# LayerNorm sums by ones matmuls, a convolution block projected one place earlier, and the transposes of y in another kind of PSUM bank

## The chip, the cores and the metric

One core of a Trainium2 chip. The metric is device microseconds of one execution of the whole program. Engines are named as in the profile: PE (TensorE matmuls; PEld its weight loads), DVE (VectorE), ACT (ScalarE), POOL (GpSimd), SP (SyncE). The kernel before takes 1667.99 us, median of 3 runs (1667.68 to 1668.74).

## The reference, cut to what matters

```python
u = rmsnorm(h, norm_mix_w)                      # h: 16 meta tokens + 512 tokens, 1024 wide
z, xbc, dt_raw, conf_in = split(u @ w_in)       # ONE input projection
y_ssd = ssd_mixer(z, xbc, dt_raw, ...)          # conv of 4 taps, chunked scan, gate, RMSNorm by group
a, g = split(conf_in, 2)
c = causal_depthwise_conv(a * sigmoid(g), conf_conv_w, conf_conv_b)     # 31 taps, 1024 channels
mu = mean(c, axis=-1); var = mean((c - mu) ** 2, axis=-1)               # over the 1024 channels
y_conf = silu((c - mu) * rsqrt(var + EPS) * ln_g + ln_b)                # LayerNorm, swish
h = h + concatenate([y_ssd, y_conf]) @ w_out    # ONE output projection
h = h + peer_ffn(rmsnorm(h, norm_ffn_w), ...)   # 8 heads, top 16 of 128 x 128 single-neuron experts
out = rmsnorm(h, norm_final_w)[16:]
```

All arrays are float32.

## The kernel before, in words

Every matmul operand is split in a high and a low part, and a product is three matmuls, `mm3` (L160, L161, L162: high by high, high by low, low by high). The input projection is cut into 20 blocks that go over PE in the order of the string `ORDER`: `z0` to `z3` (gates of the SSD groups), `x0` to `x7` (x, B and C of the SSD), `c0` to `c7` (the 8 blocks of 128 channels of the convolution branch). As soon as the blocks of an SSD group are there, `ssd(g)` is written, ahead of other work (priority 2000); it works in PSUM banks of the kind "pb" (4 of them), the projection in banks of the kind "pa" (4).

`c_block(k)` projects block k in two halves (272 and 256 columns each), forms the GLU on ACT and DVE (L415, L416), and runs the 31 taps as 30 DVE instructions of 128x512 (L422), written with low priority. A copy of the mean of block 0 (`crow`) is subtracted from each block (L424); block 0's mean over channels comes from 4 ones matmuls (L428): the block's 128x128 pieces are the weights, and one column of ones is what moves through. The LayerNorm needs, for each token, the sum over all 1024 channels of the block values and of their squares. Blocks 0 to 6 are added up by DVE, in `sumd` (L439) and `sumq` (L438), 128x512 each; the squares are made by ACT (L436). At the end, in the part that begins at L679 (priority 500), 16 ones matmuls (L683) reduce `sumd`, `sumq`, block 7 and block 7's square over partitions; L685 to L693 turn that into the factors, `to_rows` (L402) spreads them over the partitions, and for each block DVE (L704, L705) and ACT (L706 Silu, L707 copy) make the normalised rows that the output projection reads.

The output projection `out_part(bs)` runs over the 4 quarters of w_out's rows, in two halves of columns (hf): `out_part([0])`, `out_part([1])` for the SSD's half, `out_part([2, 3])` for the convolution's. A quarter and half is 16 `mm3` of 512 columns (48 matmuls), in 4 "pa" banks by token tile t; L660 adds a finished bank to `h1`. Its weights come through `wsplit`: ACT copies the high part (L184) and its negative (L185) into one of two slots, and a DMA that POOL issues (L186) adds the raw weights onto it, which leaves the low part. Slots are used in turn, so the weights of `[1]`, hf 0 go into the slot that `[0]`, hf 0 has read. The y of the SSD comes back from DRAM (`yD`, issued by SP) and is transposed on PE by `y_split` (L620) into a "pa" bank; ACT (L626) and DVE (L627) split it.

The order on each engine is made when the program is built, by a scheduler that goes by priorities and its own cost estimates; on the chip each engine takes its instructions in that order, and waits for what the next one needs.

Of the kernel before, what the change touches and what calls it, by code (L numbers as in the profile page):

```python
# [15 lines left out]
AF = mybir.ActivationFunctionType  # L16
OP = mybir.AluOpType
# [4 lines left out]
D = 1024  # L22
# [18 lines left out]
NT = 4  # L41
HOLD = 2
TB = 8
ORDER = "z0 c0 x4 c1 x5 x6 c2 x7 x0 z1 x1 c3 c4 z2 x2 c5 z3 x3 c6 c7".split()
YP = 300
MO = (0, 1, -1, 2, 3)

# [65 lines left out]
F0 = S0 + 9728  # L113
L0 = F0 + 4240
# [3 lines left out]
def body(ctx, tc, I, out):  # L118
    nc = tc.nc
    V, S, G, E = nc.vector, nc.scalar, nc.gpsimd, nc.tensor  # L120
# [7 lines left out]
    def ps(tag="pb"):  # L128
        return psp.tile([128, 512], F32, name=tag, tag=tag)

    def early(n):
        return tc.high_priority(offset=n)

    def late(n):
        return tc.high_priority(offset=-n)

    def mem(a, n):
        assert a + n <= SLAB
        return M[:, a:a + n]
# [7 lines left out]
    def con(n):  # L147
        a = cp[0]
        cp[0] += n
        assert cp[0] <= W0, cp[0]  # L150
        return M[:, a:a + n]
# [64 lines left out]
    raws = []  # L216
    worder = [{"z": k - 1, "x": 3 + k, "c": 11 + k}[o] for o, k in ((o[0], int(o[1])) for o in ORDER) if (o, k) != ("z", 0)]

    def next_w():
        while worder and len(raws) < 2:  # L220
            src = I["win"][worder.pop(0)].rearrange("p j c n -> p (j c n)")
            raws.append((wload(src), src))
        raw, src = raws.pop(0)
        return wsplit(raw, src, parts=2)
# [10 lines left out]
    ones = con(128)  # L235
# [12 lines left out]
    def stat(n):  # L248
        a = stp[0] % 128
        if a + n > 128:  # L250
            a = 0
        stp[0] = a + n
        return st[:, a:a + n]

    def rstd_of(ss, n, scale, parts=128):
        v = stat(n)[:parts]
        V.tensor_scalar(v, ss, scale, EPS, op0=OP.mult, op1=OP.add)  # L257
        r = stat(n)[:parts]
        G.tensor_tensor(r, v, neghalf[:parts, :n], op=OP.pow)  # L259
        return r  # L260
# [11 lines left out]
    dtraw = con(80)  # L272
# [19 lines left out]
    for n, t in enumerate(MO):  # L292
        src, c0, parts = (xt[t], NM + 128 * t, 128) if t >= 0 else (xm, 0, NM)
# [6 lines left out]
        for half in range(2):  # L300
            hs = slice(512 * half, 512 * half + 512)
            V.scalar_tensor_tensor(u[:, hs], src[:parts, hs], r, wmix[:parts, hs], op0=OP.mult, op1=OP.mult)
            p = ps("pa" if n % 2 else "pb")
# [8 lines left out]
    def proj_ct(wh, wl, j):  # L312
        p0, p1 = ps("pa"), ps("pa")
        for dc in range(8):
            sh = wh[:, j * 1024 + dc * 128:j * 1024 + dc * 128 + 128]
            sl = wl[:, j * 1024 + dc * 128:j * 1024 + dc * 128 + 128]
            f, l = dc == 0, dc == 7
            mm3(p0[:, :272], sh, sl, uTh[:, dc, 0:272], uTl[:, dc, 0:272], f, l)
            mm3(p1[:, :256], sh, sl, uTh[:, dc, 272:528], uTl[:, dc, 272:528], f, l)
        return p0, p1  # L320
# [64 lines left out]
    convo = mem(V0, 4096).rearrange("p (c t) -> p c t", c=8)  # L385
    glu = [mem(F0 + 544 * k, 544) for k in range(4)]
    sig = mem(F0 + 2176, 528)
    atmp = [mem(F0 + 2704 + 512 * k, 512) for k in range(2)]
    cwh = con(248)
    V.tensor_scalar(cwh, small[:, S_CW:S_CW + 248], 0.5, None, op0=OP.mult)  # L390
    crow = mem(L0, 512)
    sumd = mem(L0 + 512, 512)
    sumq = mem(L0 + 1024, 512)
    assert L0 + 1536 <= SLAB
    ccol = con(4)
    atn = [0]
    sq7 = []

    def to_rows(cols):
        p = ps()  # L400
        for t in range(4):
            E.matmul(p[:, 128 * t:128 * t + 128], cols[:, t:t + 1].to_broadcast([128, 128]), ident,  # L402
                     start=True, stop=True)
        return p

    def c_block(k):
        wh, wl = next_w()
        g0, g1 = proj_ct(wh, wl, 0)
        S.activation(sig[:, 0:272], g0[:, :272], AF.Tanh, scale=0.5)
        S.activation(sig[:, 272:528], g1[:, :256], AF.Tanh, scale=0.5)  # L410
        a0, a1 = proj_ct(wh, wl, 1)
        gl = glu[k % 4]
        if k < 4:
            V.memset(gl[:, 0:14], 0.0)
        V.scalar_tensor_tensor(gl[:, 14:286], sig[:, 0:272], 1.0, a0[:, :272], op0=OP.add, op1=OP.mult)  # L415
        V.scalar_tensor_tensor(gl[:, 286:542], sig[:, 272:528], 1.0, a1[:, :256], op0=OP.add, op1=OP.mult)  # L416
        o = convo[:, k, :]
        cw = cwh[:, 31 * k:31 * k + 31]
        with late(LOWP):
            S.activation(o, gl[:, 0:512], AF.Identity, scale=cw[:, 0:1], bias=small[:, S_CB + k:S_CB + k + 1])  # L420
            for j in range(1, 31):
                V.scalar_tensor_tensor(o, gl[:, j:j + 512], cw[:, j:j + 1], o, op0=OP.mult, op1=OP.add)  # L422
            if k > 0:
                V.tensor_tensor(o, o, crow, op=OP.subtract)  # L424
            if k == 0:
                p = ps()
                for t in range(4):
                    E.matmul(p[:, t:t + 1], o[:, 128 * t:128 * t + 128], ones[:, 0:1], start=True, stop=True)  # L428
                V.tensor_scalar(ccol, p[:, 0:4], 1.0 / 128, None, op0=OP.mult)
                S.activation(crow, to_rows(ccol), AF.Copy)  # L430
                V.tensor_tensor(o, o, crow, op=OP.subtract)
                S.activation(sumq, o, AF.Square)
            else:
                at = atmp[atn[0] % 2]
                atn[0] += 1
                S.activation(at, o, AF.Square)  # L436
                if k < 7:
                    V.tensor_tensor(sumq, sumq, at, op=OP.add)  # L438
                    V.tensor_tensor(sumd, convo[:, 0, :] if k == 1 else sumd, o, op=OP.add)  # L439
                else:  # L440
                    sq7.append(at)


    sm = con(80 * 12)
# [144 lines left out]
    left = [0, 1, 2, 3]  # L589
    for o in ORDER:  # L590
        {"z": z_block, "x": x_block, "c": c_block}[o[0]](int(o[1]))
# [10 lines left out]
    def hl(kk):  # L602
        g = RG[kk // 4]
        return g[0][:, kk % 4, :], g[1][:, kk % 4, :]
# [10 lines left out]

    def y_split(src, t, g0, n):
        ts = slice(128 * t, 128 * t + 128)
        p = ps("pa")
        for d in range(2 * n):
            E.transpose(p[:, d * 128:d * 128 + 128], src[:, d * 128:d * 128 + 128], ident)  # L620
        for d in range(2 * n):
            kk = 2 * g0 + d
            wc = small[:, S_NW + kk:S_NW + kk + 1]
            pd = p[:, d * 128:d * 128 + 128]
            hh, ll = hl(kk)
            S.activation(hh[:, ts], pd, AF.Copy, scale=wc)  # L626
            V.scalar_tensor_tensor(ll[:, ts], pd, wc, hh[:, ts].bitcast(F32), op0=OP.mult, op1=OP.subtract)  # L627
# [49 lines left out]


    with early(LNP):  # L679
        p = ps()  # L680
        for c0, src in ((0, sumd), (4, sumq), (8, convo[:, 7, :]), (12, sq7[0])):
            for t in range(4):
                E.matmul(p[:, c0 + t:c0 + t + 1], src[:, 128 * t:128 * t + 128], ones[:, 0:1], start=True, stop=True)  # L683
        mom = stat(8)
        V.tensor_scalar(mom, p[:, 0:8], 1.0 / D, None, op0=OP.mult)  # L685
        V.scalar_tensor_tensor(mom, p[:, 8:16], 1.0 / D, mom, op0=OP.mult, op1=OP.add)
        dl = mom[:, 0:4]
        vv = stat(4)
        V.tensor_tensor(vv, dl, dl, op=OP.mult)
        V.tensor_tensor(vv, mom[:, 4:8], vv, op=OP.subtract)  # L690
        rst = rstd_of(vv, 4, 1.0)
        rho = stat(4)
        V.tensor_tensor(rho, dl, rst, op=OP.mult)  # L693
        prh = to_rows(rho)
        prs = to_rows(rst)
        pin = tc.keep_in_program_order

        def low(k):
            ch, cl = hl(k)
            pin(V.tensor_tensor(cl, convo[:, k, :], ch.bitcast(F32), op=OP.subtract))  # L700

        for k in range(8):
            cv = convo[:, k, :]
            pin(V.tensor_tensor(cv, cv, prs, op=OP.mult))  # L704
            pin(V.tensor_tensor(cv, cv, prh, op=OP.subtract))  # L705
            S.activation(cv, cv, AF.Silu, bias=small[:, S_LB + k:S_LB + k + 1], scale=small[:, S_LG + k:S_LG + k + 1])  # L706
            S.activation(hl(k)[0], cv, AF.Copy)  # L707
            if k > 1:
                low(k - 2)
        low(6)  # L710
        low(7)
# [4 lines left out]
    for t in range(4):  # L716
        x2 = x2s if t == 3 else mem(P0 + 1024 + 1024 * (t % 2), 1024)
# [107 lines left out]
    for h in range(8):  # L825
        wh, wl = split_n(raw_n(I["wq"][h].rearrange("p c n -> p (c n)"), 2048), 2048, V)
        for f in range(2):
            pq = ps("pa")
            for dc in range(8):
                o = dc * 256 + f * 128  # L830
# [4 lines left out]
            for t in range(4):  # L835
                E.matmul(psc[:, 128 * t:128 * t + 128], qT[:, 128 * t:128 * t + 128], keys[:, 2 * h + f, :],
                         start=True, stop=True)
# [258 lines left out]
```

## Time and profile before

| | us |
|---|---|
| runs (3): lowest, median, highest | 1667.68, 1667.99, 1668.74 |
| the profiled execution: its own time | 1670.01 |
| its span (first to last instruction) | 1668.2 |
| PE busy | 1619.8 (97%) |
| DVE busy | 1396.2 (84%) |
| ACT busy | 772.9 (46%) |
| POOL busy | 397.4 (24%) |
| mean granted TensorE clock | 0.988 |

Times in the trace count from the span's start. A timeline row gives start, duration, engine, line, operation, its output and input, and the count; in brackets stands the time that the engine sat idle before it and who released it. Several equal instructions in a row are one line; a matmul of plain float32 operands (the ones matmuls) stands there as two instructions, a transpose as one. The duration of a pipelined instruction is longer than the distance to the next one's start, which is the price used here. Granted clock 1.00 is 2.4 GHz, 0.50 is 1.2 GHz. The input projection fills about the first 298 us, the SSD's tail and the output projection follow to about 430 us, and the retrieval takes the rest.

### The profile page before, as it was taken

Reading aid. Unit: us, or ns where it says so; the run is one execution under the profiler, and the core shown is the slowest. Engines: PE = TensorE matmul, PEld = TensorE weight load, DVE = VectorE, ACT = ScalarE, POOL = GpSimd, SP = SyncE. Lnnn points to the kernel's source line nnn. Section 1 sums busy time; section 2 is a strip of 40 time slices with the busy share of each in tenths; the row PEclk is TensorE's granted clock in tenths of the full one; section 3 lists DMA queues with packets and bytes.
Section 4 is the critical chain, followed back from the end, with each engine's and each line's share of the span. In section 5 each row is a group of like instructions: output and inputs, shape, how many; then the busy total and the mean of one; then the engine's idle time right before and its main releaser. Section 6 shows DMA issues by size and latency. Waiting matters only on the chain. (4 is left out here: it accounts for less than half of the span.)

```text
span 1668.2 us, 26169 instructions
## 1 busy us (share of the span) xinstructions
PE 1619.8 (97%) x9529; PEld 1470.6 (88%) x9529; DVE 1396.2 (84%) x2864; ACT 772.9 (46%) x1179; POOL 397.4 (24%) x348
## 2 busy tenths in 40 slices
PE   7999999888899999999999999999999999999997
PEld 7999999767788999999999988888888899999996
DVE  5999899994579999999997478888888788988876
ACT  5566566536333344676766333333333333333332
POOL 1111111012000012022223232222222355454430
PEclk9999999988999999999999999999999999999999
DMA  7877576656222466799998889999999899999982
GB/s 218 191 169 170 130 162 156 201 132 143 82 92 80 136 190 233 221 338 340 331 332 316 293 291 367 348 344 349 349 337 350 303 343 354 355 357 361 338 309 89
DMA packets 166913, 425.38 MB, mean 255 GB/s; under 512 B 14576, under 2 KB 81392, under 8 KB 161664
## 3 DMA queue, kind: packets, MB, share of 16 engines
q1 hardware_dynamic: 121568, 261.17, 45.1%
q0 software_dynamic: 45216, 162.55, 32.2%
q8 instruction: 74, 1.21, 0.3%
q14 instruction: 55, 0.45, 0.1%
HBM read 381.72 MB, written 41.94 MB: 254 GB/s over the span
## 5 line engine op out<-in xcount | busy, mean ns | idle before, releaser
L160 PE MATMUL pa<-MR 128*128 128x512 f32 (+3 forms) x2120 | 726.9, 344 | 9.0 <-ACT MR L707 3.0
L161 PE MATMUL pa<-MR 128*128 128x512 f32 (+3 forms) x2120 | 726.2, 343 | 0.0
L162 PE MATMUL pa<-MR 128*128 128x512 f32 (+3 forms) x2120 | 687.7, 344 | 1.2 <-DVE MR L267 1.1
L160 PEld LDWEIGHTS pa<-MR 128*128 128x128 f32 x2120 | 402.1, 190 | 40.1 <-ACT MR L707 3.3
L162 PEld LDWEIGHTS pa<-MR 128*128 128x128 f32 x2120 | 401.3, 189 | 32.2 <-DVE MR L267 1.3
L161 PEld LDWEIGHTS pa<-MR 128*128 128x128 f32 x2120 | 401.8, 190 | 30.0 <-DVE MR L267 0.5
L788 ACT ACTIVATE MR<-M 128x1024 fp32r<-128x1024 f32 (+1 forms) x264 | 286.0, 1084 | 294.3 <-PE pa L161 107.1
L789 DVE TENSOR_TENSOR MR<-M,MR 128x1024 fp32r<-128x1024 f32 (+1 forms) x264 | 330.6, 1254 | 75.0 <-ACT MR L788 70.1
L929 POOL DMA_INDIRECT M<-wd,M x128 | 160.7, 1256 | 545.6 <-DVE M L945 280.3
L929 POOL DMA_INDIRECT M<-wu,M x128 | 164.0, 1281 | 313.9 <-DVE M L952 269.9
L161 PE MATMUL pb<-MR 128*128 128x384 f32 (+1 forms) x576 | 206.8, 359 | 0.0
L160 PE MATMUL pb<-MR 128*128 128x384 f32 (+1 forms) x576 | 206.3, 359 | 0.0
L162 PE MATMUL pb<-MR 128*128 128x384 f32 (+1 forms) x576 | 204.2, 359 | 0.0
L1016 ACT ACTIVATE MR<-M 128x384 fp32r<-128x384 f32 x128 | 67.0, 523 | 272.9 <-issue 203.2
L422 DVE SCALAR_TENSOR_TENSOR M<-M 128x512 f32<-128x512 f32 x240 | 174.5, 750 | 3.9 <-ACT M L420 3.0
L952 DVE SCALAR_TENSOR_TENSOR M<-M 128x1024 f32<-128x1024 f32 x128 | 163.8, 1279 | 14.0 <-DMA M<-wu,M 13.8
L945 DVE SCALAR_TENSOR_TENSOR M<-M 128x1024 f32<-128x1024 f32 x128 | 154.1, 1219 | 9.6 <-DMA M<-wd,M 9.6
L1017 DVE TENSOR_TENSOR MR<-M,MR 128x384 fp32r<-128x384 f32 x128 | 71.2, 556 | 59.6 <-ACT MR L1016 58.9
L160 PEld LDWEIGHTS pb<-MR 128*128 128x128 f32 x576 | 108.1, 188 | 11.4
L161 PEld LDWEIGHTS pb<-MR 128*128 128x128 f32 x576 | 108.1, 188 | 11.3
L162 PEld LDWEIGHTS pb<-MR 128*128 128x128 f32 x576 | 108.1, 188 | 10.7
L991 ACT ACTIVATE M<-pb 128x512 f32<-128x512 f32 x96 | 99.0, 1160 | 37.5 <-PE pb L989 37.5
(221 smaller groups left out, 1494.3 us busy)
## 6 DMA issues: line engine op xcount, KB each, us to landing
M<-wdT SPq DMA_DIRECT2D x128, 512.0 KB
M<-wu SPq DMA_DIRECT2D x128, 512.0 KB
GD<-M SPq DMA_DIRECT2D x40, 512.0 KB
M<-GD SPq DMA_DIRECT2D x32, 640.0 KB
M<-win SPq DMA_DIRECT2D x19, 1024.0 KB
MR<-win POOLq DMA_DIRECT2D x38, 512.0 KB
HD<-M SPq DMA_DIRECT2D x88, 192.0 KB
M<-HD SPq DMA_DIRECT2D x88, 192.0 KB
```

Of the source, the lines that this page charges most:

```text
L160: E.matmul(o, lh, rh, start=first, stop=False)
L161: E.matmul(o, lh, rl, start=False, stop=False)
L162: E.matmul(o, ll, rh, start=False, stop=last)
L422: V.scalar_tensor_tensor(o, gl[:, j:j + 512], cw[:, j:j + 1], o, op0=OP.mult, op1=OP.add)
L788: S.activation(wh, raw, AF.Copy)
L789: leng.tensor_tensor(wl, raw, wh.bitcast(F32), op=OP.subtract)
L929: r = G.indirect_dma_start(out=g, out_offset=None, in_=src, in_offset=bass.IndirectOffsetOnAxis(ap=e3[:, k:k + 1], axis=0))
L945: use(V.scalar_tensor_tensor(g, g, 1.0, x2s, op0=OP.mult, op1=OP.mult, accum_out=dots[:, k:k + 1]))
L952: use(V.scalar_tensor_tensor(h1[3], g, act3[:, k:k + 1], h1[3], op0=OP.mult, op1=OP.add))
L991: S.activation(gb.rearrange("p i t -> p t i")[:, c:c + 4, :], p.rearrange("p (t i) -> p t i", t=4), AF.Copy, scale=1.0 / GS)
L1016: S.activation(sh, sf, AF.Copy)
L1017: V.tensor_tensor(sl, sf, sh.bitcast(F32), op=OP.subtract)
```

## The change

Three edits. `c2` stands one place earlier in `ORDER`, ahead of `x6`. The 12 DVE adds (L438, L439) go: `block_sums(k)` reduces each block and its square by 8 ones matmuls into one column each, and a small DVE instruction adds the 128x8 result into `mom`; it is written two blocks later, in `c_block(k + 2)`, for blocks 0 to 5, and at the LayerNorm for 6 and 7. Four buffers for the squares instead of two take the place of `sumd` and `sumq`. `y_split` transposes into a "pb" bank. Lines behind the edits shift: L402 is now L399, L415 L412, L422 L419, L436 L429, L706 L701, L707 L702; the ones matmul is L437, its DVE instructions L439 and L441.

```diff
-ORDER = "z0 c0 x4 c1 x5 x6 c2 x7 x0 z1 x1 c3 c4 z2 x2 c5 z3 x3 c6 c7".split()
+ORDER = "z0 c0 x4 c1 x5 c2 x6 x7 x0 z1 x1 c3 c4 z2 x2 c5 z3 x3 c6 c7".split()
...
-    atmp = [mem(F0 + 2704 + 512 * k, 512) for k in range(2)]
+    atmp = [mem(o, 512) for o in (F0 + 2704, F0 + 3216, L0 + 512, L0 + 1024)]
...
-    sumd = mem(L0 + 512, 512)
-    sumq = mem(L0 + 1024, 512)
+    mom = dtraw[:, 0:8]
...
-                S.activation(sumq, o, AF.Square)
-            else:
-                at = atmp[atn[0] % 2]
-                atn[0] += 1
-                S.activation(at, o, AF.Square)
-                if k < 7:
-                    V.tensor_tensor(sumq, sumq, at, op=OP.add)
-                    V.tensor_tensor(sumd, convo[:, 0, :] if k == 1 else sumd, o, op=OP.add)
-                else:
-                    sq7.append(at)
+            S.activation(atmp[k % 4], o, AF.Square)
+            if k > 1:
+                block_sums(k - 2)
+
+    def block_sums(k):
+        p = ps()
+        for c0, src in ((0, convo[:, k, :]), (4, atmp[k % 4])):
+            for t in range(4):
+                E.matmul(p[:, c0 + t:c0 + t + 1], src[:, 128 * t:128 * t + 128], ones[:, 0:1], start=True, stop=True)
+        if k == 0:
+            V.tensor_scalar(mom, p[:, 0:8], 1.0 / D, None, op0=OP.mult)
+        else:
+            V.scalar_tensor_tensor(mom, p[:, 0:8], 1.0 / D, mom, op0=OP.mult, op1=OP.add)
...
     def y_split(src, t, g0, n):
         ts = slice(128 * t, 128 * t + 128)
-        p = ps("pa")
+        p = ps("pb")
...
     with early(LNP):
-        p = ps()
-        for c0, src in ((0, sumd), (4, sumq), (8, convo[:, 7, :]), (12, sq7[0])):
-            for t in range(4):
-                E.matmul(p[:, c0 + t:c0 + t + 1], src[:, 128 * t:128 * t + 128], ones[:, 0:1], start=True, stop=True)
-        mom = stat(8)
-        V.tensor_scalar(mom, p[:, 0:8], 1.0 / D, None, op0=OP.mult)
-        V.scalar_tensor_tensor(mom, p[:, 8:16], 1.0 / D, mom, op0=OP.mult, op1=OP.add)
+        block_sums(6)
+        block_sums(7)
```

The new order moves instructions in three places. The first is PE at the end of the input projection (L160 to L162 with 272 and 256 columns are the last matmuls of block c7's projection, L536 to L563 the SSD's). Before, transposes of y (L620) stand between the projection's matmuls:

```order
L162 MATMUL pa<-MR 128x256
L620 MATMUL pa<-M 128x128 x2
L160 MATMUL pa<-MR 128x272
L620 MATMUL pa<-M 128x128 x2
L161 MATMUL pa<-MR 128x272
...
L563 MATMUL pb<-M 128x256
L536 MATMUL pb<-M 128x128
L561 MATMUL pb<-M 128x64 x4
```

Of the changed kernel, what stands behind the projection and the SSD's last attention matmuls but two, down to the output projection's first matmuls:

```order
L437 MATMUL pb<-M 128x1 x16
L559 MATMUL pb<-M 128x256
L561 MATMUL pb<-M 128x64 x4
L620 MATMUL pb<-M 128x128 x6
L160 MATMUL pa<-MR 128x512
L161 MATMUL pa<-MR 128x512
```

All transposes of y now come behind the whole projection, and two blocks' ones matmuls (16 instructions) stand ahead of the first of them. Ahead of c7's last projection matmul there are 32 more ones matmuls than before, 4 transposes fewer, and 14 matmuls of the SSD (2 of L536, 1 L539, 4 L542, 1 L559, 4 L561, 2 L563) that stood behind it before.

The second place is PE in the output projection. The number behind `pa` is the bank's generation. Before, `[0]`, hf 1 ends (pa_3661), the transposes for quarter 1 follow, and then `[1]`, hf 0 begins (pa_3778), 48 matmuls after the last matmul that reads the weights of `[0]`, hf 0:

```order
L160 MATMUL pa_3661<-MR_64 128x512
L161 MATMUL pa_3661<-MR_64 128x512
L162 MATMUL pa_3661<-MR_64 128x512
L620 MATMUL pa_3719<-M_63 128x128 x2
...
L620 MATMUL pa_3771<-M_63 128x128 x2
L160 MATMUL pa_3778<-MR_64 128x512
L161 MATMUL pa_3778<-MR_64 128x512
```

Now the last matmul of `[0]`, hf 0 (into pa_3649) stands in the third quarter of hf 1 (pa_3706 to pa_3709), and the first of `[1]`, hf 0 is pa_3826:

```order
L161 MATMUL pa_3708<-MR_64 128x512
L162 MATMUL pa_3649<-MR_64 128x512
L162 MATMUL pa_3708<-MR_64 128x512
...
L620 MATMUL pb_3791<-M_63 128x128 x2
L620 MATMUL pb_3798<-M_63 128x128 x2
L620 MATMUL pb_3805<-M_63 128x128 x2
L160 MATMUL pa_3709<-MR_64 128x512
...
L160 MATMUL pa_3826<-MR_64 128x512
L160 MATMUL pa_3827<-MR_64 128x512
```

33 matmuls stand from hf 1's first one to the one into pa_3649, and 20 matmuls and 10 transposes behind it before the low part of `[1]`'s weights is needed. From there to the LayerNorm's spreading matmuls there are 80 matmuls with 512 columns and 16 ones matmuls, and 12 more matmuls behind the spreading.

The third place is ACT at the LayerNorm. Before, the squares (L436), splits of quarter 2 (L184, L185), the load of the table for Silu (L706), and then pairs of Silu and copy:

```order
L184 ACTIVATE MR<-M 128x512
L185 ACTIVATE MR<-MR 128x512 x2
L706 ACT_TABLE_LOAD
L706 ACTIVATE M<-M 128x512
L707 ACTIVATE MR<-M 128x512
L706 ACTIVATE M<-M 128x512
```

Now splits of quarter 3, whose slot is that of `[1]`, hf 1, stand ahead of the table load, between it and the first copy:

```order
L185 ACTIVATE MR<-MR 128x512 x2
L184 ACTIVATE MR<-M 128x512 x2
L185 ACTIVATE MR<-MR 128x512
L701 ACT_TABLE_LOAD
L701 ACTIVATE M<-M 128x512
L184 ACTIVATE MR<-M 128x512
L185 ACTIVATE MR<-MR 128x512
L184 ACTIVATE MR<-M 128x512
L701 ACTIVATE M<-M 128x512
L702 ACTIVATE MR<-M 128x512
```

The two L184 in one row wait for the first matmuls of the 12 behind the spreading. From the first matmuls of `out_part([2, 3])` on, the order of PE and DVE is the same in both kernels, down to the end of the program.

## Rows read from the trace of the kernel before

**Rows 1.** Busy time by stretches of the span (start and end, length; of each engine its busy time and the number of instructions; granted clock, share of the DMA engines, GB/s).

```profile
24.00:280.00 256.00, 256.00 (x2100) 251.28 (x2100) 224.17 (x427) 152.38 (x299) 39.09 (x46) 1.00 0.70 160
...
320.00:340.00 20.00, 19.89 (x98) 16.24 (x96) 20.00 (x41) 8.16 (x15) 1.99 (x3) 1.00 0.53 150
340.00:360.00 20.00, 12.31 (x42) 9.10 (x43) 20.00 (x43) 8.55 (x21) 1.45 (x2) 0.74 0.44 106
```

**Rows 2.** The longest of PE's waits from 395 us to the end (its instruction, the releaser; us in total, times, the longest).

```profile
PE pb L611 <- DVE M L724: 4.4, 1, 4.4
```

**Rows 3.** PE timeline from the ones matmuls of block 0 on (4 in the program, 8 in the records), inside a projection block.

```profile
92.07 0.95 PE L428 MATMUL pb<-M 128*128 128x1 f32 x8
92.88 0.37 PE L161 MATMUL pa<-MR 128*128 128x272 f32 x1
93.09 0.29 PE L162 MATMUL pa<-MR 128*128 128x272 f32 x1
```

**Rows 4.** PE timeline at the end of c7's projection, and the DVE row that takes its result.

```profile
297.03 0.44 PE L620 MATMUL pa<-M 128*128 128x128 f32 x2 [1.53 <-DMA M<-yD]
297.22 0.37 PE L160 MATMUL pa<-MR 128*128 128x272 f32 x1
...
298.20 0.28 PE L162 MATMUL pa<-MR 128*128 128x256 f32 x1
```

```profile
298.16 0.44 DVE L415 SCALAR_TENSOR_TENSOR M<-M,pa 128x272 f32<-128x272 f32 x1 [0.57 <-PE pa L162]
```

**Rows 5.** DVE timeline: adds of the sums with an instruction of 256 columns between them, a run of taps, splits of y with the row behind them.

```profile
162.44 0.69 DVE L439 TENSOR_TENSOR M<-M 128x512 f32<-128x512 f32 x1
163.04 0.41 DVE L573 TENSOR_TENSOR M<-M,pb 128x256 f32<-128x256 f32 x1
163.38 0.69 DVE L438 TENSOR_TENSOR M<-M 128x512 f32<-128x512 f32 x1
...
253.26 4.05 DVE L422 SCALAR_TENSOR_TENSOR M<-M 128x512 f32<-128x512 f32 x6
...
342.38 0.88 DVE L627 SCALAR_TENSOR_TENSOR MR<-pa,M,MR 128x128 fp32r<-128x128 f32 x3
343.15 1.42 DVE L422 SCALAR_TENSOR_TENSOR M<-M 128x512 f32<-128x512 f32 x2
```

**Rows 6.** PE timeline in the output projection: the spacing of 512-column matmuls, and the rows before which PE was idle.

```profile
324.79 0.39 PE L160 MATMUL pa<-MR 128*128 128x512 f32 x1
325.01 0.39 PE L161 MATMUL pa<-MR 128*128 128x512 f32 x1
...
345.21 0.69 PE L620 MATMUL pa<-M 128*128 128x128 f32 x2 [3.90 <-DVE MR L627]
...
350.59 0.79 PE L160 MATMUL pa<-MR 128*128 128x512 f32 x1 [2.53 <-DVE MR L627]
```

**Rows 7.** The split of a quarter's weights on ACT and POOL, and the DMA share by single microseconds behind it (columns as in rows 1).

```profile
327.02 1.92 ACT L184 ACTIVATE MR<-M 128x2048 fp32r<-128x2048 f32 x1 [2.00 <-PE pa L162]
328.98 1.92 ACT L185 ACTIVATE MR<-MR 128x2048 fp32r<-128x2048 f32 x1
...
341.09 0.86 ACT L626 ACTIVATE MR<-pa,M 128x128 fp32r<-128x128 f32 x3
```

```profile
331.19 0.89 POOL L186 DMA_DIRECT2D MR<-wout  x1 [1.56 <-ACT MR L185]
```

```profile
332.00:333.00 1.00, 1.00 (x10) 0.96 (x9) 1.00 (x3) 0.51 (x2) 0.08 (x1) 1.00 1.06 442
...
338.00:339.00 1.00, 1.00 (x6) 0.83 (x5) 1.00 (x2) 0.00 (x0) 0.00 (x0) 1.00 0.26 49
```

**Rows 8.** The LayerNorm's chain, by engine: PE, DVE, ACT.

```profile
376.34 1.84 PE L683 MATMUL pb<-M 128*128 128x1 f32 x16
381.33 3.75 PE L402 MATMUL pb<-M 128*128 128x128 f32 x16 [3.15 <-DVE M L693]
388.10 0.50 PE L160 MATMUL pa<-MR 128*128 128x512 f32 x1 [3.01 <-ACT MR L707]
```

```profile
373.39 0.69 DVE L424 TENSOR_TENSOR M<-M 128x512 f32<-128x512 f32 x1
...
381.02 0.16 DVE L693 TENSOR_TENSOR M<-M 128x4 f32<-128x4 f32 x1 [1.83 <-POOL M L259]
385.12 0.69 DVE L704 TENSOR_TENSOR M<-M,pb 128x512 f32<-128x512 f32 x1 [3.93 <-PE pb L402]
```

```profile
378.16 1.13 ACT L185 ACTIVATE MR<-MR 128x512 fp32r<-128x512 f32 x2
379.31 1.28 ACT L706 ACT_TABLE_LOAD   x1
386.57 0.81 ACT L706 ACTIVATE M<-M 128x512 f32<-128x512 f32 x1 [5.98 <-DVE M L705]
387.41 0.63 ACT L707 ACTIVATE MR<-M 128x512 fp32r<-128x512 f32 x1
```

**Rows 9.** Short stretches after PE's waits, with the granted clock (columns as in rows 1).

```profile
350.00:355.00 5.00, 4.41 (x10) 3.47 (x11) 5.00 (x12) 0.37 (x1) 0.00 (x0) 0.50 0.27 56
...
389.00:392.00 3.00, 3.00 (x9) 2.37 (x8) 2.96 (x6) 2.58 (x5) 0.00 (x0) 0.52 0.01 1
```

**Rows 10.** DVE between the end of c2's taps (at 160 us) and the arrival of c3's projection (at 179 us).

```profile
173.08 0.43 DVE L567 TENSOR_TENSOR M<-M 128x256 f32<-128x256 f32 x1 [1.66 <-PE pb L559]
```

More of the change, by code (lines that the diff above doesn't have):

```diff
@@ L391, in body @@
     crow = mem(L0, 512)
-    sumd = mem(L0 + 512, 512)
-    sumq = mem(L0 + 1024, 512)
+    mom = dtraw[:, 0:8]
     assert L0 + 1536 <= SLAB
     ccol = con(4)
-    atn = [0]
-    sq7 = []
     def to_rows(cols):
```

## The prediction

> **What bounds the kernel now.** I read the busy time by stretches first. From 24 to 280 us PE is busy in 256.00 of 256 us at clock 1.00, DVE in 224 of them [rows 1]: the projection is PE's, and an instruction added there moves everything behind it. From 320 us the picture turns. DVE is busy 20.00 of 20 us in two stretches running, and PE falls to 12.31 in the second, with the clock at 0.74 [rows 1]. PE's timeline names the waits: 3.90 and 2.53 us for L627, the split of y on DVE [rows 6]. The LayerNorm then follows as a chain: 3.15 us for the factors (L693), 3.01 us for the first normalised rows (L707), and the second half of the output projection starts at 388.10 [rows 8]. From 395 us to the end PE's longest wait is 4.4 us [rows 2]; it hangs on the same results in both kernels, and the order behind that start is unchanged. So the change is worth what it does to the 388.10. I follow that time through five steps.
>
> **Step 1, the end of the projection.** Four ones matmuls take 0.81 us, 92.07 to 92.88, so 0.20 each; the projection matmul behind them hands over after 0.21 where its neighbours of that kind take 0.12, so 0.09 for each return to the other kind [rows 3]. The order puts 32 more of them ahead of c7's last projection matmul, in 23 more places: 32 x 0.20 + 23 x 0.09 = 8.5. Fourteen SSD matmuls come ahead too; at the price of a ones matmul, the nearest row, 2.8. Four transposes leave, 0.19 for two [rows 4]: -0.4. The 1.53 us that a transpose waited there for yD [rows 4] goes with them. Sum: +9.4. The last projection matmul started at 298.20 [rows 4] and now starts at about 307.6. No cover exists, since PE is full, and DVE waits for it: L415 already stood idle 0.57 us for that result [rows 4].
>
> The 12 adds that go are worth 0.60 each on DVE (162.44 to 163.04; with the 0.34 of the row between them, 163.38) [rows 5], 7.2 together; six small DVE instructions come in at 0.2 (the 0.16 row of L693 [rows 8]): -6.0. Most of these lie ahead of c7's arrival. There DVE only waits longer, so I give them nothing.
>
> The move of `c2` I cost at nothing. It brings one block of taps to DVE earlier, but DVE was idle there waiting for PE anyway, 1.66 us at 173.08 for one [rows 10], and the idle time moves to another place; the cover that counts is PE's full row. Its weight load on SP and its two L186 on POOL change places with x6's, which are of the same size. Without that cover a shift of c2 could only show again at c7, which is step 1. The bank of the transposes has no price that a row shows: it could give back the projection's waits for a "pa" bank (none stands in PE's 256.00 of 256), and it may cost what its place in the order costs, steps 2 and 3. I take it with these.
>
> **Step 2, DVE from c7's arrival to the first finished bank.** All y splits are now behind the projection. Between c7's L412 and the first L660 DVE has 76 instructions: 30 taps x 0.67 (4.05 for 6), 15 splits x 0.26 (0.77 for 3), and 31 others between 0.2 and 0.6, mostly the 0.34 of 256 columns [rows 5], 9.8 together. That is 33.8 us. L412 starts at 298.16 + 9.4 = 307.6, so the last split ends at 341.4; three matmuls (0.7) and the hand-overs (0.6, an estimate from the 0.33 between the last projection matmul of that half and L415) follow, and the L660 ends near 343.4. In the meantime PE has only transposes and part of quarter 0 to do.
>
> **Step 3, the weights of quarter 1.** Hf 1 cannot begin before that bank is free. 33 matmuls at 0.22 to 0.23 (324.79 to 325.01) [rows 6] are 7.5, so the last reader of the slot ends at 351. Then ACT's L184 1.9, three L626 0.8, L185 1.9, and the DMA from its issue at 331.19 to where its share falls away within 338 to 339, 7.0 [rows 7]: the low part lands at about 363. Before, 48 matmuls (10.9 us) stood behind that point. Now 20 matmuls and 10 transposes do, 4.6 + 1.2, and PE runs dry near 357: a new wait of about 6 us. Queued behind the waiting matmul are all of quarter 1 and the LayerNorm's ones matmuls; on POOL, the LayerNorm's L259 stands behind 4 weight DMAs where 7 stood, which takes nothing.
>
> **Step 4, to the spreading matmuls.** 80 matmuls (18.2), 16 ones matmuls (16 x 0.20 + 0.2 = 3.4), the 8 spreading matmuls (1.6 at the same price), and the clock. After each such wait the rows show PE at half clock, 0.50 over 350 to 355 and 0.52 over 389 to 392 [rows 9]; the work of 3.0 to 4.4 busy us then takes 1.5 to 2.2 longer, I take 1.8. 363 + 25.0 = 388.0 for the end of the spreading, T; before it was 385.08 (381.33 + 3.75 [rows 8]). The 3.15 wait for the factors is gone: 32 matmuls (7.3 us) now stand between the last ones matmuls and the spreading, against 3 us from 378 to 381 [rows 8]. The price of a ones matmul by the other row, 1.84 for 8 [rows 8], would add 1.0 in all of steps 1 and 4.
>
> **Step 5, to the first matmul of quarters 2 and 3.** Before, 3.0 us. Now ACT, in order, has two L184 for quarter 3 that wait for the first 6 of the 12 matmuls behind the spreading (1.4), then 0.6 for the second of them and 0.6 for an L185 (1.13 for two), the table load 1.28, Silu 0.84 (386.57 to 387.41), three splits at 0.6, a second Silu 0.84, and the first copy 0.63 [rows 8]: 8.0. Start: 388.0 + 8.0 = 396.0, 7.9 later.
>
> The profiled execution's own time is 1670.01, 1.8 above its span and 2.0 above the median of the runs; 7.9 on it gives 1677.9, and on the median 1675.9, which is what I forecast.
>
> A page bears on step 5. The table load's row shows 1.28 us, with ACT idle behind it for L705 [rows 8], so a tail of the load could hide there. The Trainium skill, page "ScalarE: Activation LUTs", section "What ACT_TABLE_LOAD costs", puts a switch at about 1283 ns for the load and 1380 ns for a drain, 2.66 us in all; by it the sum, in which nothing covers the load any more, would be 1.4 higher, 1677.3. The trace agrees on the load and can't show the drain. I leave it out of the sum.
>
> **Rivals.** R1, faster: DVE, not PE, sets the end. Then its ledger of -6.0 counts in full, the 3.15 wait is covered, and nothing of step 1 arrives: 1662.0. For it speaks DVE's 20.00 of 20 from 320 to 360 [rows 1]; against it, that c7's projection was already awaited (0.57). It decides if the last projection matmul comes less than about 3 us later, so if the 32 ones matmuls cost PE a third of what rows 3 say.
>
> R2, no difference: step 1 happens, but the split of step 3 is ready in time, because the last matmul of `[0]`, hf 0 comes earlier or the DMA is quick, so its 6 us and the clock's 1.8 go: T = 380.2, start 388.2, 1668.1. Against it speak the 7.0 us of the DMA [rows 7] and the 48 matmuls that have become 20.
>
> R3, slower still: the raw load of quarter 3, which ACT's next L184 sets free at about 358, runs beside that DMA. While a load and that DMA ran together, the share was 1.06 at 442 GB/s [rows 7]; 1.05 MB at this rate is 2.4 us on the accumulating DMA. With one more stretch at half clock (1.8), from PE's long wait between 310 and 343, the start is at 400.2, 1680.1. A page states the ground for it: the Trainium skill, "DMA: Bandwidth & Descriptors", section "Issuing engines are not separate DMA queues", says that transfers started by different engines run on the same 16 DMA engines and interleave. By it the 2.4 is paid wherever the two meet; the trace agrees so far as its share of 1.06 in that microsecond goes.
>
> That the adds don't go, or that the matmuls don't come, the order excludes.
>
> **How the numbers follow.** Forecast 1675.9: chance 0.52, own range 1671.5 to 1680 (down, the switches at nothing, -2.1, and a third of step 3's wait covered, -2; up, the higher price of ones matmuls, 1.0, R3's 2.4 and some of its clock). R3 0.12; R2 0.18; R1 0.18. Within 0.2% (about what a measurement of this kernel can tell from no change) is 1664.7 to 1671.3. Slower has the forecast and R3, less a little of the forecast's low end that R2 gains: 0.62; the same 0.20; faster 0.18. The range for 8 in 10 reaches from 1664.5, which leaves out most of R1, to 1683, R3 with the 1.0 of the ones matmuls and one more stretch at half clock.
>
> **What would show it.** Step 1: c7's L162 at 306 to 309, ones matmuls in groups at 0.20 each, PE full to there. Step 2: first L660 at 342 to 345, PE idle in several pieces for L627 between 310 and 340. Step 3: a wait of PE of 4 to 8 us for the DMA of L186 around 357 to 363. Step 4: no wait at L399 for the factors. Step 5: the table load behind L185 after the spreading, and the first matmul of quarters 2 and 3 at 394 to 400. Behind it PE's rows should be as before, shifted. The prediction is wrong if c7's projection ends before 302, or if PE finds the weights of quarter 1 in place.

## The result, and the profile after

The changed kernel takes 1680.11 us, median of 4 runs (1679.14 to 1680.95), beside 1668.37 for the kernel before (4 runs): a ratio of 1.0061, 95% interval 1.0049 to 1.0072. It is slower by about 10 us; the forecast was 1675.9, in a range of 1664.5 to 1683.

| | before | after |
|---|---|---|
| the profiled execution, us | 1670.01 | 1679.14 |
| its span | 1668.2 | 1677.4 |
| PE busy | 1619.8 | 1631.4 |
| DVE busy | 1396.2 | 1390.2 |
| mean granted clock | 0.988 | 0.988 |

PE has 11.6 us more work and DVE 6.0 less, about what the diff says: 48 ones matmuls in, 12 adds out, six small DVE instructions in. By stretches, as [rows 1]:

```profile
24.00:280.00 256.00, 256.00 (x2104) 251.44 (x2104) 221.88 (x429) 152.18 (x302) 40.06 (x47) 1.00 0.68 157
...
320.00:340.00 20.00, 19.71 (x92) 16.20 (x93) 20.00 (x47) 8.81 (x26) 1.54 (x2) 0.85 0.18 53
340.00:360.00 20.00, 13.30 (x62) 10.36 (x60) 19.96 (x42) 11.37 (x17) 1.75 (x2) 0.92 0.48 123
360.00:380.00 20.00, 18.62 (x87) 15.78 (x88) 8.19 (x16) 5.02 (x9) 3.46 (x5) 0.82 0.51 129
```

In 360 to 380 DVE is busy 8.19 of 20 us (15.54 before): it no longer holds PE up there. The waits that count are in PE's timeline; the rows below answer to [rows 4, 6, 8]: the end of c7's projection, the last matmul of `[0]`, hf 0 (one of the two at 346.79), the last wait for a split of y, the first matmul that needs the low part of quarter 1's weights, the LayerNorm's spreading matmuls, and the first matmul of quarters 2 and 3.

```profile
304.45 0.28 PE L162 MATMUL pa<-MR 128*128 128x256 f32 x1
...
346.79 0.62 PE L162 MATMUL pa<-MR 128*128 128x512 f32 x2
...
354.57 0.44 PE L620 MATMUL pb<-M 128*128 128x128 f32 x2 [1.29 <-DVE MR L627]
361.38 0.80 PE L161 MATMUL pa<-MR 128*128 128x512 f32 x1 [6.38 <-DMA MR<-wout]
...
385.86 1.95 PE L399 MATMUL pb<-M 128*128 128x128 f32 x16
...
395.35 0.79 PE L160 MATMUL pa<-MR 128*128 128x512 f32 x1 [4.79 <-ACT MR L702]
```

A wait of 6.38 us for quarter 1's weights is new. Of the waits of 3.90 and 2.53 us for L627 [rows 6] one of 1.29 is left. The 3.15 us wait at the spreading is gone, and the wait behind it has grown from 3.01 to 4.79 [rows 8]. What leads to the 6.38, on ACT and POOL:

```profile
347.22 1.92 ACT L184 ACTIVATE MR<-M 128x2048 fp32r<-128x2048 f32 x1 [4.65 <-PE pa L162]
349.04 0.87 ACT L626 ACTIVATE MR<-pb,M 128x128 fp32r<-128x128 f32 x3
349.79 1.93 ACT L185 ACTIVATE MR<-MR 128x2048 fp32r<-128x2048 f32 x1
```

```profile
352.01 0.89 POOL L186 DMA_DIRECT2D MR<-wout  x1 [17.83 <-ACT MR L185]
356.64 0.86 POOL L186 DMA_DIRECT2D MR<-wout  x1 [3.73 <-ACT MR L626]
```

The split begins when the slot's last reader is done, and its DMA takes from 352.01 to 361.38, 9.4 us, where [rows 7] show 7.0. A second one, for the next half, is issued at 356.64 while the first still runs. Raw weights for later quarters are loaded too, issued by SP at 349.16 and about 353.5; beside the DMA of [rows 7] there was one such load, issued at 328.97.

What stands ahead of the 4.79, on ACT:

```profile
388.54 1.33 ACT L184 ACTIVATE MR<-M 128x512 fp32r<-128x512 f32 x2 [10.04 <-PE pa L162]
389.77 0.61 ACT L185 ACTIVATE MR<-MR 128x512 fp32r<-128x512 f32 x1
390.40 1.28 ACT L701 ACT_TABLE_LOAD   x1
391.70 0.81 ACT L701 ACTIVATE M<-M 128x512 f32<-128x512 f32 x1
...
394.68 0.61 ACT L702 ACTIVATE MR<-M 128x512 fp32r<-128x512 f32 x1
```

From 395 us on, PE runs at half clock for six more microseconds; in the kernel before it was three [rows 9]. Behind that the two kernels run alike, with the same longest wait as [rows 2].

```profile
395.00:398.00 3.00, 2.65 (x6) 2.15 (x7) 2.38 (x4) 3.00 (x7) 1.53 (x2) 0.50 0.94 279
398.00:401.00 3.00, 3.00 (x8) 2.30 (x7) 2.93 (x6) 1.54 (x4) 0.20 (x1) 0.50 0.89 159
...
PE pb L611 <- DVE M L719: 4.4, 1, 4.4
```

Two profiled executions can't be laid over each other from zero. The granted clock between 12 and 24 us was 0.86 in the one of before and 1.00 in the one of after, and block 0's ones matmuls, which both have, start at 92.07 and at 90.53. I therefore count from these. From there to c7's last projection matmul: 206.1 us before, 213.9 after, +7.8. To the matmuls of the second RMSNorm (L611 with the 4.4 us wait): 347.6 and 357.5, +9.9. To the end: 1576.1 and 1586.9, +10.7. So all but about 1 us of the loss is made ahead of 448 us. What follows that wait takes 1228.5 and 1229.4 us in these two; over all the runs below it takes 1226.3 to 1230.6. A difference of 2 us in one profiled execution is therefore not yet one of the kernels.

### The profile page after: what moved, and what is told of

Same layout as the page of the kernel before. It is cut to its first block, busy times and chain, and to the rows that moved or that the text cites. A ratio compares the mean times of both kernels' runs of the same rounds, so it can differ in the third digit from the quotient of the medians.

```text
span 1677.4 us, 26347 instructions
## 1 busy us (share of the span) xinstructions
PE 1631.4 (97%) x9625; PEld 1481.2 (88%) x9625; DVE 1390.2 (83%) x2858; ACT 773.2 (46%) x1179; POOL 398.6 (24%) x348
## 5 line engine op out<-in xcount | busy, mean ns | idle before, releaser
L160 PE MATMUL pa<-MR 128*128 128x512 f32 (+3 forms) x2120 | 727.1, 344 | 8.8 <-ACT MR L702 4.8
L162 PE MATMUL pa<-MR 128*128 128x512 f32 (+3 forms) x2120 | 687.2, 344 | 1.7 <-DVE MR L267 1.2
L160 PEld LDWEIGHTS pa<-MR 128*128 128x128 f32 x2120 | 401.7, 190 | 40.2 <-ACT MR L702 5.2
L162 PEld LDWEIGHTS pa<-MR 128*128 128x128 f32 x2120 | 400.6, 189 | 33.1 <-DVE MR L267 1.4
L160 PE MATMUL pb<-MR 128*128 128x384 f32 (+1 forms) x576 | 206.3, 359 | 0.0
L162 PE MATMUL pb<-MR 128*128 128x384 f32 (+1 forms) x576 | 204.2, 359 | 0.0
L419 DVE SCALAR_TENSOR_TENSOR M<-M 128x512 f32<-128x512 f32 x240 | 172.5, 743 | 1.6 <-ACT M L417 0.9
L161 PEld LDWEIGHTS pb<-MR 128*128 128x128 f32 x576 | 108.1, 188 | 11.6 <-DVE MR L784 0.3
L160 PEld LDWEIGHTS pb<-MR 128*128 128x128 f32 x576 | 108.1, 188 | 11.3
L162 PEld LDWEIGHTS pb<-MR 128*128 128x128 f32 x576 | 108.1, 188 | 10.7
```

The source lines that it names most:

```text
L160: E.matmul(o, lh, rh, start=first, stop=False)
L161: E.matmul(o, lh, rl, start=False, stop=False)
L162: E.matmul(o, ll, rh, start=False, stop=last)
```

## The experiments

Each was timed in 5 rounds beside the kernel before, in three groups. "To c7" and "to L611" are the two stretches just named, in the profiled execution, and the next column is PE's longest wait for a DMA of quarter 1's weights.

| run | what | ratio to before, 95% | to c7 | to L611 | wait for weights |
|---|---|---|---|---|---|
| before | | | 206.1 | 347.6 | none |
| after | all three edits | 1.0061 (1.0049, 1.0072) | 213.9 | 357.5 | 6.38 |
| e1 | sums alone | 0.9996 (0.9987, 1.0004) | 216.2 | 346.6 | none |
| e2 | bank alone | 1.0033 (1.0020, 1.0045) | 203.9 | 353.2 | 0.34 |
| e3 | c2 alone | 1.0001 (0.9991, 1.0011) | 204.6 | 347.1 | none |
| e4 | sums and bank | 1.0018 (1.0008, 1.0028) | 214.2 | 348.0 | 2.69 |
| e5 | sums and c2 | 1.0013 (1.0004, 1.0021) | 214.4 | 347.9 | none |
| e6 | after, quarters 0 and 1 in chunks | 0.9986 (0.9978, 0.9995) | 213.9 | 348.4 | 0.54 |
| e7 | after, Silu first | 1.0057 (1.0044, 1.0070) | 213.9 | 358.0 | 6.27 |
| e8 | after, groups 0 and 1 in pa | 1.0000 (0.9990, 1.0010) | 214.4 | 348.3 | none |
| e9 | before, quarters 0 and 1 in chunks | 1.0006 (0.9995, 1.0016) | 207.9 | 351.0 | none |
| e10 | after, one split in chunks | 0.9999 (0.9990, 1.0008) | 213.9 | 346.7 | 0.85 |
| e11 | sums alone, in chunks | 1.0005 (0.9995, 1.0015) | 214.6 | 351.9 | none |
| e12 | sums alone, ones matmuls twice | 1.0092 (1.0071, 1.0113) | 225.1 | 362.0 | none |

**The three edits apart.** e1 is the changed kernel with two edits undone:

```diff
-ORDER = "z0 c0 x4 c1 x5 c2 x6 x7 x0 z1 x1 c3 c4 z2 x2 c5 z3 x3 c6 c7".split()
+ORDER = "z0 c0 x4 c1 x5 x6 c2 x7 x0 z1 x1 c3 c4 z2 x2 c5 z3 x3 c6 c7".split()
...
-        p = ps("pb")
+        p = ps("pa")
```

> The sums by ones matmuls alone; order of the blocks and bank of the transposes as before. Theory A (ones matmuls push c7's projection back by about 9 us, DVE's 6 us less work gives part of it back; the rest of the loss is the lost cover of quarter 1's weights and the splits of quarter 3 ahead of the Silu): here the last reader of the slot stands 49 matmuls ahead of the low part, as before, so no wait of PE for the DMA of quarter 1's weights; c7's last projection matmul at 306 to 308; +1 to +4 us, about 1671. Rival C (PE is the bound throughout, and the 48 added ones matmuls cost their 11 us wherever they stand): +11, about 1679. Rival B (the ones matmuls are covered; the bank makes the loss): 0 or faster.

```profile
308.24 0.47 PE L162 MATMUL pa<-MR 128*128 128x256 f32 x1
```

c7's projection came 10 us later, and the end was level with before: rival B's number, below the +1 to +4 of theory A. PE's busy time rose by 9.8 us (1629.6), so rival C falls: added work of PE isn't paid in full. It went into waits that PE has anyway behind the projection: from block 0's ones matmuls to L611 PE's busy time grew from 322.7 to 332.2 us, and its idle time shrank from 24.9 to 14.4.

e2 is the kernel before with this alone:

```diff
-        p = ps("pa")
+        p = ps("pb")
```

> The transposes of y in a pb bank alone; sums and order of the blocks as before. Theory A: the transposes move behind c7's projection, but the last reader of the slot still stands 50 matmuls ahead of the low part: -2 to +2 us, about 1668. Rival C: 0. Rival B: most of the 11.7 us, about 1678, with a wait of several us for quarter 1's weights.

It cost 5.5 us (0.0033 of 1669), more than theory A allowed, and without the wait that rival B names. c7's projection is 2 us earlier, but the output projection's first matmul comes at 322.96, where before it stood at 312.51:

```profile
321.85 0.66 PE L620 MATMUL pb<-M 128*128 128x128 f32 x2 [1.69 <-issue]
322.96 0.80 PE L160 MATMUL pa<-MR 128*128 128x512 f32 x1 [0.46 <-ACT MR L626]
...
310.00:320.00 10.00, 6.25 (x24) 4.37 (x22) 10.00 (x21) 2.04 (x7) 0.66 (x1) 0.50 0.16 37
320.00:330.00 10.00, 7.25 (x24) 4.98 (x23) 10.00 (x22) 3.70 (x11) 0.99 (x1) 0.51 0.23 91
```

PE has 6.25 and 7.25 us of work in 10, at half clock, where before it had 9.17 and 10.00 at 0.97 and 1.00: the matmuls of quarter 0 that filled these gaps before have to wait for y. So the bank has a price of its own, in another place than the one I forecast, and neither A nor B had its size.

e3 is the kernel before with the new `ORDER` alone:

```diff
-ORDER = "z0 c0 x4 c1 x5 x6 c2 x7 x0 z1 x1 c3 c4 z2 x2 c5 z3 x3 c6 c7".split()
+ORDER = "z0 c0 x4 c1 x5 c2 x6 x7 x0 z1 x1 c3 c4 z2 x2 c5 z3 x3 c6 c7".split()
```

> c2 ahead of x6 alone; sums and bank as before. All theories: no change, within 1 us of before; DVE's idle time between c2 and c3 only moves, and c7's last projection matmul stays at 298 us.

Level, as expected.

e4 is the changed kernel with `ORDER` put back, so that the sums and the bank stay:

```diff
-ORDER = "z0 c0 x4 c1 x5 c2 x6 x7 x0 z1 x1 c3 c4 z2 x2 c5 z3 x3 c6 c7".split()
+ORDER = "z0 c0 x4 c1 x5 x6 c2 x7 x0 z1 x1 c3 c4 z2 x2 c5 z3 x3 c6 c7".split()
```

> The changed kernel with c2 back behind x6. Here 39 matmuls stand between the last reader of the slot and the low part of quarter 1's weights (49 before, 20 in the changed kernel). Theory A: the wait for these weights falls from 6.4 to 1 to 3 us, c7's projection is as late as in the changed kernel (306 to 308); +4 to +8 us, about 1674. Rival C: +11, about 1679, as the changed kernel. Rival B: as the changed kernel, about 1680.

The loss is 3.0 us, less than the +4 to +8 expected, and 7 less than the changed kernel's. The cover is about half of these 7: with 39 matmuls the wait is 2.69 us, with 20 it is 6.38, and the spreading starts 4.2 us earlier here. The first matmul of quarters 2 and 3 comes 8.2 earlier: all of quarter 1 stands ahead of the spreading here, and ACT has quarter 3's splits done by 385.88, just behind it. e3 and e4 together say that moving c2 costs nothing by itself and 7 us on top of the other two; it does so through the order that the scheduler then writes down.

**Which part carries the loss.** e5 puts the bank back and keeps the sums and c2's place:

```diff
-        p = ps("pb")
+        p = ps("pa")
```

> The changed kernel with the transposes of y back in a pa bank. Theory A2 (the bank is what carries the loss: transposes in pb can only be placed behind the last SSD group's banks, which pushes the output projection's first quarter back, and c2's move costs only by the order that the scheduler then makes): 49 matmuls cover the split of quarter 1 again, no wait for its weights; 0 to +2 us on before, about 1670. Rival D (c2's move and the ones matmuls together cost, whatever the bank): +6 to +8, about 1676.

+0.13%, 2.2 us, just over the upper end of what A2 gave, and far from rival D. e8 goes half of this way:

```diff
-        p = ps("pb")
+        p = ps("pa" if g0 < 2 else "pb")
```

> The changed kernel with the transposes of groups 0 and 1 back in pa, and those of groups 2 and 3 left in pb. Theory A2: the first transposes are again free of the SSD's banks, so this goes like the kernel with all of them in pa: 0 to +2 us on before, about 1670. Rival E (it is the late groups, whose transposes take pb banks from the LayerNorm's sums and the SSD's end): as the changed kernel, about +10, 1679.

Level with before. So, beside the other two edits, it is the transposes of groups 0 and 1, the first ones, that must not stand in "pb"; those of 2 and 3 may. That the "pb" banks come round to them only behind the last SSD group is how I read the order; no run shows that reason by itself.

**The wait for quarter 1's weights.** e6 is the changed kernel with

```diff
-                ws.append(wsplit(wload(src), src, parts=4 if len(bs) > 1 else 1))
+                ws.append(wsplit(wload(src), src, parts=4))
```

> The changed kernel with the weights of quarters 0 and 1 split in 4 chunks, as quarters 2 and 3 are; only the last chunk then waits for the slot's last reader, the first three are ready earlier. If the 6.4 us wait for quarter 1's weights is on the path that sets the end: the wait falls under 2 us and the whole by 3 to 5 us on the changed kernel, to +6 to +7 on before, about 1675. If another wait takes its place: no change, +10.

The wait fell to 0.54, and the whole by three times what I expected: 2.3 us below the kernel before. Everything up to c7 is as in the changed kernel, 213.9 to the tenth. The 2.3 are not won here, though: at L611 this kernel is 0.8 us behind the kernel before. 2.0 of them stand at the very end. From the end of the last DVE instruction to the end of the span it takes 3.6 us in the three kernels with all splits in chunks (e6, e9, e11), 6.1 in e10 and 5.6 in all the others; below, that instruction in the kernel before (span 1668.2) and in e6 (1666.0). No edit here is about this stretch, and why it is shorter stays open.

```profile
1661.23 1.41 DVE L1069 SCALAR_TENSOR_TENSOR M<-M 128x512 f32<-128x512 f32 x2 [0.66 <-POOL M L259]
1661.01 1.41 DVE L1064 SCALAR_TENSOR_TENSOR M<-M 128x512 f32<-128x512 f32 x2 [0.73 <-POOL M L259]
```

e9 is the control, the same edit on the kernel before:

> The kernel before, with the weights of quarters 0 and 1 split in 4 chunks. If the chunks only remove the changed kernel's wait (theory A3: the single-piece split behind a late last reader is what the change ran into), the kernel before, where 49 matmuls cover the split, gains nothing: within 1.5 us of before. If the chunks are worth something by themselves (rival F: the changed kernel with chunks is fast because of the chunks everywhere): -5 or more.

Nothing is gained there, so rival F falls; at L611 this execution is even 3.4 us later, and 2.0 come back at the end. e10 narrows it to one split, in the changed kernel:

```diff
-                ws.append(wsplit(wload(src), src, parts=4 if len(bs) > 1 else 1))
+                ws.append(wsplit(wload(src), src, parts=4 if len(bs) > 1 or (b, hf) == (1, 0) else 1))
```

> The changed kernel, with only the split of quarter 1, columns half 0, in 4 chunks; the other 3 single-piece splits of quarters 0 and 1 as they were. Theory A3: this split alone carries the wait; as with all of them in chunks, -2 to +2 us on before, about 1668 to 1670. Rival F (the chunks of quarter 0 matter too): half of the way or less, +5 or more.

Level with before: this one split gives back 10 us. The wait of 0.85 that is left is for quarter 1's other half, still split in one piece. PE's rows:

```profile
367.04 0.50 PE L161 MATMUL pa<-MR 128*128 128x512 f32 x1 [0.85 <-DMA MR<-wout]
...
380.86 2.05 PE L399 MATMUL pb<-M 128*128 128x128 f32 x16 [0.86 <-DVE M L688]
385.92 0.80 PE L160 MATMUL pa<-MR 128*128 128x512 f32 x1 [3.01 <-ACT MR L702]
```

Counted from block 0's ones matmuls (92.06 here), the spreading starts at 288.8 and quarters 2 and 3 at 293.9; in the changed kernel 295.3 and 304.8. So 6.5 us of the difference are there at the spreading, although 12 more matmuls stand ahead of it here: the wait, and the half clock behind it (0.51 from 361.38 to 367.10 in the changed kernel, 1.00 here from 340 to 380). 4.4 more come between the spreading and the next quarter. The second part is an order too: here all of quarter 1 stands ahead of the spreading, quarter 3's slot is free in time, and ACT splits it while it waits for the factors. The edit made the scheduler write a new order, so no run takes the wait alone away and leaves the rest as it was; the two parts are read from the traces.

ACT's rows here:

```profile
380.94 1.13 ACT L185 ACTIVATE MR<-MR 128x512 fp32r<-128x512 f32 x2
382.09 1.28 ACT L701 ACT_TABLE_LOAD   x1
384.39 0.81 ACT L701 ACTIVATE M<-M 128x512 f32<-128x512 f32 x1 [1.02 <-DVE M L700]
385.24 0.63 ACT L702 ACTIVATE MR<-M 128x512 fp32r<-128x512 f32 x1
```

**The Silu behind the splits.** e7 makes quarter 3's splits wait for the first normalised row, by a factor of 1 computed from it:

```diff
+            if k == 0:
+                V.tensor_scalar(hold, hl(k)[0][:, 0:1].bitcast(F32), 0.0, 1.0, op0=OP.mult, op1=OP.add)
...
-            S.activation(wh[:, js], raw[:, js], AF.Copy)
+            S.activation(wh[:, js], raw[:, js], AF.Copy, scale=scale)
```

> The changed kernel, with the splits of quarter 3 (columns half 0) made to wait for the first normalised row by a scale of exactly 1 that is computed from it (one small DVE instruction more); the order on all engines up to there is unchanged. If step 5 is right (ACT's splits ahead of the Silu set the start of quarters 2 and 3): the wait at that start falls from 4.8 to about 1 us, the whole by 3 to 4.5 us on the changed kernel, +6 to +7 on before, about 1675. If the time comes back as a wait for quarter 3's weights: -1 or nothing.

The wait did fall, from 4.79 to 0.26, and nothing came of it:

```profile
393.54 0.50 PE L160 MATMUL pa<-MR 128*128 128x512 f32 x1 [0.26 <-ACT MR L704]
...
397.37 1.21 PE L162 MATMUL pa<-MR 128*128 128x512 f32 x4 [1.71 <-DVE MR L697]
400.78 0.79 PE L160 MATMUL pa<-MR 128*128 128x512 f32 x1 [2.20 <-ACT MR L704]
```

The four splits now stand between the first normalised row and the second, and PE waits 1.71 and 2.20 us there, then goes to half clock (0.51 from 400 to 403). ACT has the same work to do in the same place, whichever row comes first. In e10 it had done it earlier.

**The price of a ones matmul.** e11 asks whether the sums can be made to pay: e1 with all splits in chunks.

> The sums by ones matmuls, order of the blocks and bank as before, and the weights of quarters 0 and 1 in 4 chunks: the candidate to beat both kernels. Sums alone were level with before, chunks took the changed kernel to 2 us below before. If DVE's 6 us less work can come through once no weights are waited for: -2 to -4 us, about 1666. If PE's 11 us more work or the LayerNorm's chain holds the end: 0.

They can't; level in time, and in the profiled execution 4.3 us late at L611. e12 issues each ones matmul twice, into the same column, and halves the constant:

```diff
-                E.matmul(p[:, c0 + t:c0 + t + 1], src[:, 128 * t:128 * t + 128], ones[:, 0:1], start=True, stop=True)
+                E.matmul(p[:, c0 + t:c0 + t + 1], src[:, 128 * t:128 * t + 128], ones[:, 0:1], start=True, stop=False)
+                E.matmul(p[:, c0 + t:c0 + t + 1], src[:, 128 * t:128 * t + 128], ones[:, 0:1], start=False, stop=True)
```

> The sums by ones matmuls alone, each ones matmul issued twice (64 matmuls more, 13 us of PE by 0.20 each; the doubled sums are halved by the constant): prices PE's work in the projection. Rival C (PE's added work counts in full): +13 on before. Theory A3: the sums alone were free because PE's waits behind the projection took 10 us up; of the second 13 us about half has no wait left to hide in: +4 to +9, about 1675.

+15.4 us (0.0092 of 1670) for 64 matmuls, 0.24 each: more than theory A3's +4 to +9 and a little over rival C's 13, in an order that the scheduler again made anew. That they come near their price is in part chance. PE's busy time is 18.8 us above e1's (1648.4 and 1629.6), with more of it at half clock (0.61 from 320 to 340 and 0.59 from 360 to 380, where e1 has 0.74 and 0.88), and its idle time ahead of L611 fell by 4.5 more, to 9.9. The first 48 cost nothing at the end and the next 64 about their price: what added work can hide in is bounded, and the first 48 used most of it up.

## Why the prediction was right, and where its steps were not

The forecast, slower by 7.9 us, has the right sign and most of the size; the measured 10.2 us lies between it and rival R3's 12.1. (As a bare time 1680.11 is R3's 1680.1, but the kernel before was at 1668.37 beside it and not at the 1667.99 that R3 starts from.)

Step 1: the last projection matmul stood at 304.45, forecast 307.6; counted from block 0's ones matmuls the delay is 7.8 us, not 9.4. That step's other half failed, that nothing covers this delay: e1 and e10 have it (10 and 7.8 us) and end level with before. I had "given nothing" for DVE's 6.0 us, because I took DVE to wait for c7. It doesn't: L412 takes c7's result at 304.61 without idle time before it, and DVE is busy 55.77 of the 55.8 us that follow. So the 6.0 count. The mean of block c6 is subtracted at 365.52 before and at 358.11 after:

```profile
365.52 0.71 DVE L424 TENSOR_TENSOR M<-M 128x512 f32<-128x512 f32 x1
358.11 0.69 DVE L421 TENSOR_TENSOR M<-M 128x512 f32<-128x512 f32 x1
```

Counted from block 0's ones matmuls that is 273.5 and 267.6, 5.9 earlier, in spite of c7's delay. PE's added work in turn stands where PE waited before, for L627 and for the factors, as e1's idle time shows. R1's ledger of DVE was right, as the other side of step 1 rather than as a rival to it; its 1662.0 was not reached by any run.

Step 2: the first L660 came at 337.93, 33.5 us behind c7's last projection matmul, as the 76 instructions said. It ended at 338.61, 4.8 us before my 343.4: I had started 3 too late, and most of the rest is the three matmuls and the hand-overs that I had added, for which DVE did not wait.

Step 3 is the step that carries the loss, and it held: the last reader of the slot at 347.0 (forecast 351), the weights at 361.4 (363), a wait of 6.38 (about 6). That the numbers come out so close is in part luck. In the landing the earlier reader and the DMA's 9.4 us instead of 7.0 cancelled. In the wait the longer DMA was set off by the cover, which lasted 8.0 us from the reader's end instead of 5.8, with the waits of 0.41 and 1.29 in it. The 2.4 us between 9.4 and 7.0 are as large as the price that R3 named for transfers side by side, but not all of them are that. In e4 the same DMA, with no second one beside it and the next raw load issued only at 356.6, took 8.2:

```profile
350.30 0.89 POOL L186 DMA_DIRECT2D MR<-wout  x1 [16.62 <-ACT MR L185]
358.46 0.50 PE L161 MATMUL pa<-MR 128*128 128x512 f32 x1 [2.69 <-DMA MR<-wout]
```

So far the trace agrees with the sentence of the Trainium skill, page "DMA: Bandwidth & Descriptors", section "Issuing engines are not separate DMA queues", that the prediction weighed: a transfer with neighbours took longer, by 1.2 to 2.4 us. Which neighbour it was, the raw load or the second accumulating DMA, no run separates. R3's further stretch at half clock came too (0.85 from 320 to 340, 1.00 before), but there DVE, which was never idle, set the time of the first L660.

Step 4: the spreading ended at 387.8, forecast 388.0, without a wait.

Step 5: the start at 395.35, forecast 396.0, in the very order of ACT that was priced. But the 5 us between 3.0 and 8.0 aren't what moving the Silu would give back (e7), since ACT's work sets that stretch either way. What e10 gains there, 4.4, is splits done earlier; e4, with the splits done beside the spreading, gains 4.1 there. On the table load, the Trainium skill, page "ScalarE: Activation LUTs", section "What ACT_TABLE_LOAD costs", would have 1.4 us of drain in the open here. The measurement decides against it: the Silu starts at 391.70, 0.02 us behind the load's end (390.40 + 1.28), and the load 0.02 behind the split ahead of it.

What the sum lacked: three more microseconds at half clock behind 395 (+1.1 us between the start of quarters 2 and 3 and L611), and the 1.5 us by which the two profiled executions differ ahead of block 0's ones matmuls. R2's condition, that the split is in place in time, is what e10 builds: 1668 was forecast for it, and level with before was measured, in an order of its own.

## What to carry to other kernels

Where buffers are used in turn, count the work between the last reader of a slot and the first use of what is refilled, in the order that the change makes: here 49 matmuls hid an 11 us refill, 20 left 6.4 us open, and refilling in chunks, each behind its own last reader, closed it to under 1 us. Where there was no such wait (e9, e11) chunks gained nothing. Work added to a full engine is free only as far as the same engine waits later on the same path, and that store is used up once: test it by adding more. A wait that goes isn't a gain until the next use of the engine that was waited for has been looked at.

## What the runs showed of the hardware that was not expected

An accumulating DMA of 1 MB took 7.0 us from issue to landing in the kernel before, read from the DMA share, and 8.2 in e4, read from PE's release, with one earlier raw load beside it in both. With a further load and a second such DMA beside it, it took 9.4.

The profiled executions differ by some 1.5 us before anything differs between the kernels. Block 0's ones matmuls start at 90.5 to 90.6 us in the five executions with a granted clock of 1.00 up to 90 us. They start at 91.9 to 92.2 in the eight in which it fell once, to a mean of 0.86 in 12 to 24 us or of 0.97 in 24 to 90, and at 93.4 in the one with both (e7, with 0.88 and 0.97). That alone is enough to hide a change of 0.1%.
